# Reciprocal square roots moved from VectorE to GpSimd in a two-block transformer kernel

## The chip, the cores and the metric

One core of a Trainium2 chip runs the whole kernel. The metric is the device time of one execution in microseconds (us), as the median of several runs. The engines are named as in the profile: PE is TensorE's matmul, PEld its weight load, DVE is VectorE, ACT is ScalarE, POOL is GpSimd and SP is SyncE, which here only issues DMAs. Each engine takes its instructions in one fixed order; an instruction whose input is not ready holds up all that stand behind it on the same engine.

## What is computed

Two transformer blocks on one sequence of 1024 tokens with 1024 features, in float32. The first has a hybrid mixer (a gated MLP over positions, differential attention, top-k sparse attention) and a feed-forward part of width 2816, with layer norms; the second has stick-breaking attention and a pooling mixer, the same feed-forward width, and RMS norms with a modulation. All the norms need one reciprocal square root for each token:

```
def layer_norm(x, g, b):
    mu = jnp.mean(xf, axis=-1, keepdims=True)
    xc = xf - mu
    var = jnp.mean(xc * xc, axis=-1, keepdims=True)
    return xc * lax.rsqrt(var + LN_EPS) * g + b

def rms_norm(x, g):
    ms = jnp.mean(xf * xf, axis=-1, keepdims=True)
    return xf * lax.rsqrt(ms + LN_EPS) * g
...
x = layer_norm(DEEPNORM_ALPHA * x + mix @ w_out, ln1_g, ln1_b)
ffn = (silu(gate) * up) @ w_down
x = layer_norm(DEEPNORM_ALPHA * x + ffn, ln2_g, ln2_b)
```

## The kernel before

A float32 matrix product is made of three products of a high and a low part (`mm3`, L95 to L99). A `split` (L79 to L84) makes those parts: a cast on ACT (L80) and a subtraction on DVE or POOL (L84). Tokens go in eight blocks of 128, a token to a partition. The program is handed to a scheduler, which lays out each engine's order from a timeline of its own (L1699), so taking instructions off one engine reorders others too.

`rsqrt(v, n)` (L101) takes the reciprocal root of n columns by a shift and a subtraction on the bits of the number (L105, L106), a scaling (L107) and three Newton steps (L110 and L114 for one column; L112, L113 and L114 for eight). It is called 56 times:

- eight times with eight columns, in the first 500 us: four in the gated MLP (L437), four in the differential attention (L596);
- 24 times with one column by the two layer norms and `modulate1`: `norm_stats` (L852) calls it for `layer_norm` (L863), eight for the norm after the first mixer ("norm1" below, about 595 to 695 us) and eight for the one after the first feed-forward part ("after1", about 1355 to 1450 us); in after1 `rms_scale` (L873) is called once more for each block by `modulate1` (L1245);
- 24 times with one column by `rms_scale` in the second block: two for each token block in `norm2` (L1460, about 1830 to 1950 us), one for each in `after2` (L1589, from 2584 us to the end).

What stands around it for one token block: in a layer norm a `shift` of one column (L866, DVE), the scaling of the block (L867, ACT), and a product and a sum with gain and bias (L868, L869), by the block on POOL or DVE. In `norm2` a product with a gain on POOL (L1466 for the first five blocks, L1472 for the last three), the sum with the residual on DVE (L1473), the second root, and a scaling on ACT (L1476). After that the block goes to `SAct.put` (L810): PE transposes it (L817), and the parts are split (L807 on ACT, L808 on DVE). `sums` (L829) forms differences of those parts on POOL and DVE (L834 to L836, L846, L847), which PE needs for the products of the feed-forward part. In `after2` the product with the gain is L1598, on POOL but for the last block, and the final sum is L1601 on DVE. Between the norms PE runs the products of the stage (L694 to L696 of the output projection, L97 to L99 of the feed-forward part), with their sums on DVE (L721, L1191).

Of the kernel before, what the change touches and what calls it, by code (L numbers as in the profile page):

```python
# [9 lines left out]
F32 = mybir.dt.float32  # L10
# [3 lines left out]
I32 = mybir.dt.int32  # L14
U32 = mybir.dt.uint32
AF = mybir.ActivationFunctionType
OP = mybir.AluOpType
# [6 lines left out]
P = 128  # L24
NB = S // P
# [13 lines left out]
def two_blocks(ctx: ExitStack, tc: tile.TileContext, a):  # L39
    nc = tc.nc  # L40
    V, A, T, G, DMA = nc.vector, nc.scalar, nc.tensor, nc.gpsimd, nc.sync

    cst = ctx.enter_context(tc.tile_pool(name="cst", bufs=1))
# [5 lines left out]
    def pool(name, side="left"):  # L49
        st = ExitStack()  # L50
        return st.enter_context(tc.tile_pool(name=name, bufs=1, side=side, reuse_waits="tile")), st
# [43 lines left out]
    def mm3(out, lh, ll, rh, rl, start, stop, more=False):  # L95
# [2 lines left out]
        T.matmul(out, lh, rl, start=False, stop=False, skip_group_check=more)  # L98
        T.matmul(out, ll, rh, start=False, stop=stop, skip_group_check=more)  # L99

    def rsqrt(v, n):  # L101

        y = sml.tile([P, n], F32, tag=f"rs{n}", name="rs_y")
        t = sml.tile([P, n], F32, tag=f"rt{n}", name="rs_t")
        V.tensor_single_scalar(t.bitcast(I32), v.bitcast(I32), 1, op=OP.logical_shift_right)  # L105
        V.tensor_scalar(y.bitcast(I32), t.bitcast(I32), -1.0, 1597463007.0, op0=OP.mult, op1=OP.add)  # L106
        V.tensor_single_scalar(v, v, -0.5, op=OP.mult)  # L107
        for _ in range(3):
            if n == 1:
                V.scalar_tensor_tensor(t, y, v, y, op0=OP.mult, op1=OP.mult)  # L110
            else:
                V.tensor_tensor(t, y, y, op=OP.mult)  # L112
                V.tensor_tensor(t, t, v, op=OP.mult)  # L113
            V.scalar_tensor_tensor(y, t, 1.5, y, op0=OP.add, op1=OP.mult)  # L114
        return y

    def row(t, src):
# [114 lines left out]
    def key_chunks(L):  # L232
        return (1, max(L, 256)) if L <= 512 else (2, L // 2)
# [176 lines left out]
    def gmlp_pieces():  # L410
# [10 lines left out]
        for q in range(4):  # L421
            vg = xpool.tile([P, 2, 256], F32, tag="stg", bufs=4, name="vg")
            for t in range(2):
                o = gemm_tm(wv, q * 2 + t, 256)
                with soon():
                    A.activation(vg[:, t, :], o, AF.Gelu_apprx_tanh)
            v3 = vg.rearrange("p t (g c) -> p (t g) c", c=64)
            mu = sml.tile([P, 8], F32, tag="mu", name="mu")
            V.reduce_sum(mu, v3, axis=AX.X)
            V.tensor_single_scalar(mu, mu, 1.0 / 64.0, op=OP.mult)  # L430
            V.tensor_tensor(v3, v3, mu[:, :, None].to_broadcast([P, 8, 64]), op=OP.subtract)
            sq = xpool.tile([P, 8, 64], F32, tag="stg", bufs=4, name="sqv")
            A.activation(sq, v3, AF.Square)
            va = sml.tile([P, 8], F32, tag="va", name="va")
            V.reduce_sum(va, sq, axis=AX.X)
            V.tensor_scalar(va, va, 1.0 / 64.0, LN_EPS, op0=OP.mult, op1=OP.add)
            rs = rsqrt(va, 8)  # L437
            V.tensor_tensor(v3, v3, rs[:, :, None].to_broadcast([P, 8, 64]), op=OP.mult)
            G.tensor_tensor(vg, vg, lng[:, None, :].to_broadcast([P, 2, 256]), op=OP.mult)
            G.tensor_tensor(vg, vg, lnb[:, None, :].to_broadcast([P, 2, 256]), op=OP.add)  # L440
            DMA.dma_start(vn_d[:, q * 2:q * 2 + 2, :], vg)
            yield
# [28 lines left out]
    for blk in SCORED:  # L471
        L = (blk + 1) * P
        nch, n = key_chunks(L)
# [73 lines left out]
    class LaneB:  # L547
# [30 lines left out]
        def mix(self):  # L578
            h, i = divmod(self.m, NB)
            if i == 0:  # L580
                self.vt = p1.tile([P, NB, P], F32, tag="v", bufs=1, name="vB")
                DMA.dma_start(self.vt, bv_d[:, :, h * P:(h + 1) * P])
                self.ot = p1.tile([P, NB, P], F32, tag="o", bufs=2, name="oB")
            e0, r0 = self.e.pop(self.m)
            po = probs_v(e0, i, self.vt, P, (1, 2), ps_mm)
            ot = self.ot
            V.tensor_scalar_mul(ot[:, i, :], po, r0)
            self.m += 1
            if i < NB - 1:
                return  # L590
            sq = p1.tile([P, NB, P], F32, tag="o", bufs=2, name="sqB")
            G.tensor_tensor(sq, ot, ot, op=OP.mult)
            va = sml.tile([P, NB], F32, tag="vb", name="vb")
            V.reduce_sum(va, sq, axis=AX.X)
            V.tensor_scalar(va, va, 1.0 / P, LN_EPS, op0=OP.mult, op1=OP.add)
            rs = rsqrt(va, NB)  # L596
            V.tensor_tensor(ot, ot, rs[:, :, None].to_broadcast([P, NB, P]), op=OP.mult)
            G.tensor_tensor(ot, ot, subg[:, None, :].to_broadcast([P, NB, P]), op=OP.mult)
            DMA.dma_start(mix_d[:, :, 256 + h * P:256 + (h + 1) * P], ot)
# [53 lines left out]
    accp, _ = pool("accp", "right")  # L653
# [198 lines left out]
    def norm_stats(x):  # L852

        st = sml.tile([P, 2, 6], F32, tag="bst", name="bst")
        for c in range(2):
            V.bn_stats(st[:, c, :], x[:, c * 512:(c + 1) * 512])
        mv = sml.tile([P, 2], F32, tag="mv", name="mv")
        V.bn_aggr(mv, st)
        va = sml.tile([P, 1], F32, tag="va1", name="va1")
        V.tensor_scalar_add(va, mv[:, 1:2], LN_EPS)  # L860
        return mv[:, 0:1], rsqrt(va, 1)
# [719 lines left out]
    n = 0  # L1581
# [121 lines left out]
```

## Time and profile before

| what | value |
|---|---|
| time, median of 3 runs | 2641.62 us (2641.22 to 2645.37) |
| the profiled execution's own time | 2638.86 us |
| its span in the trace | 2637.0 us |
| mean granted clock of TensorE, of full speed | 0.954 |
| PE busy | 2398.2 us, 91% |
| DVE busy | 1889.9 us, 72% (3300 instructions) |
| ACT busy | 1083.0 us, 41% |
| POOL busy | 931.7 us, 35% (550 instructions) |

The span is what the trace covers; the execution's own time is a little longer, since some start and end lies outside it. Busy shares are means over stages in which different engines are waited for, so they do not say by themselves which engine sets the time at a given place; the rows further down are of single stages.

### The profile page before, as it was taken

How to read it: one execution, taken by the hardware profiler on the slowest of the kernel's cores; microseconds unless marked ns; L12 is line 12 of the kernel's file. 1: busy time of each engine (PE TensorE's matmuls, PEld its weight loads, DVE VectorE, ACT ScalarE, POOL GpSimd, SP SyncE). 2: the span in 40 equal slices, each digit the busy share in tenths (PEclk: the TensorE clock that was granted, in tenths of full speed). 3: DMA queues.
4: the chain of work that ended last, by engine and by line, in shares of the span. 5: the costliest groups of instructions: out<-in, count | busy, mean ns of one | idle time of the engine just before them, and what ended most of it. 6: DMA issues, size and time to landing. Idle time of an engine off the chain costs nothing. (4 is left out here: it accounts for less than half of the span.)

```text
span 2637.0 us, 32552 instructions
## 1 busy us (share of the span) xinstructions
PE 2398.2 (91%) x11584; PEld 1963.6 (74%) x11584; DVE 1889.9 (72%) x3300; ACT 1083.0 (41%) x1893; POOL 931.7 (35%) x550
## 2 busy tenths in 40 slices
PE   8889897898799999989987989898879999998997
PEld 8878776787677777867866878687657788876875
DVE  4889869648866777679987366667974555548997
ACT  4559774343223223333336334445642332225332
POOL 2220233115612222356542042426361222227634
PEclk9999998999899999999998999999989999999998
DMA  5154355423254444262303524562511222214313
GB/s 181 57 150 119 115 160 168 112 83 110 97 171 135 153 168 156 86 246 80 128 16 136 163 84 139 150 180 73 183 65 57 75 80 85 76 61 175 120 66 110
DMA packets 149789, 314.32 MB, mean 119 GB/s; under 512 B 19574, under 2 KB 65654, under 8 KB 149628
## 3 DMA queue, kind: packets, MB, share of 16 engines
q1 hardware_dynamic: 139260, 293.38, 34.4%
q10 hardware_dynamic: 10368, 18.88, 1.9%
q8 instruction: 91, 1.49, 0.2%
q14 instruction: 70, 0.57, 0.1%
HBM read 230.39 MB, written 81.81 MB: 118 GB/s over the span
## 5 line engine op out<-in xcount | busy, mean ns | idle before, releaser
L940 ACT CAST wst<-tt 128x512 fp32r<-128x512 f32 x144 | 89.2, 621 | 252.7 <-PE plg L99 206.8
L941 POOL TENSOR_TENSOR wst<-rw,wst 128x512 fp32r<-128x512 f32 x51 | 74.6, 1463 | 269.2 <-ACT wst L940 97.3
L84 POOL TENSOR_TENSOR wl<-raw,wh 128x1024 fp32r<-128x1024 f32 (+2 forms) x28 | 66.9, 2393 | 243.8 <-ACT wh L80 215.2
L339 PE MATMUL plg<-qk,qk 128*128 128x384 f32 (+4 forms) x480 | 124.5, 375 | 19.9 <-DVE mn L352 6.3
L97 PE MATMUL plg<-ws,hs 128*128 128x512 f32 x288 | 114.6, 398 | 5.4 <-ACT dacc L1158 2.9
L1505 DVE TENSOR_TENSOR_SCAN sab<-sab 128x640 f32<-128x640 f32 (+7 forms) x64 | 102.0, 1599 | 19.0 <-ACT sab L1503 18.3
L280 ACT ACTIVATE junk_a<-xi,cand 128x1024 bf16<-128x1024 f32 (+1 forms) x124 | 108.8, 878 | 14.9 <-DVE cand L269 6.8
L98 PE MATMUL plg<-ws,hs 128*128 128x512 f32 x288 | 113.9, 395 | 0.0
L99 PE MATMUL plg<-ws,hs 128*128 128x512 f32 x288 | 113.8, 395 | 0.0
L941 DVE TENSOR_TENSOR wst<-tt,wst 128x512 fp32r<-128x512 f32 x144 | 107.6, 749 | 8.4 <-ACT wst L940 7.8
L339 PEld LDWEIGHTS plg<-qk,qk 128*128 128x128 f32 x480 | 81.2, 196 | 30.7 <-DVE mn L352 9.1
L84 POOL TENSOR_TENSOR hs<-hr,hs 128x1024 fp32r<-128x1024 f32 (+1 forms) x30 | 69.0, 2301 | 83.6 <-ACT hs L80 70.2
L1214 DVE SCALAR_TENSOR_TENSOR mod<-raw_c,sc,mod 128x1024 f32<-128x1024 f32 x42 | 57.6, 1371 | 54.3 <-DMA raw_c<-in_w_cond_dram 54.2
L963 DVE TENSOR_TENSOR u<-plg,u 128x512 f32<-128x512 f32 x36 | 24.8, 690 | 97.4 <-PE plg L99 97.4
L164 PE MATMUL pmm<-wh,xh 128*128 128x256 f32 (+1 forms) x320 | 91.5, 286 | 3.1 <-DVE stgl L401 1.8
L940 ACT CAST wst<-rw 128x512 fp32r<-128x512 f32 x77 | 47.6, 618 | 111.1 <-PE plg L99 56.8
L353 ACT ACTIVATE e<-e,mn 128x128 f32<-128x128 f32 (+7 forms) x96 | 74.1, 773 | 46.1 <-DVE mn L352 42.3
L165 PE MATMUL pmm<-wl,xh 128*128 128x256 f32 (+1 forms) x320 | 90.5, 283 | 0.0
L166 PE MATMUL pmm<-wh,xl 128*128 128x256 f32 (+1 forms) x320 | 90.5, 283 | 0.0
L989 POOL TENSOR_TENSOR u<-u,u 128x512 f32<-128x512 f32 x36 | 54.9, 1526 | 92.6 <-issue 54.9
L80 ACT CAST wh<-raw 128x1024 fp32r<-128x1024 f32 x54 | 56.4, 1047 | 72.1 <-PE pmm L98 28.2
L694 PE MATMUL pmm<-woh,mixh 128*128 128x512 f32 x192 | 79.9, 416 | 6.6 <-DVE rs_t L110 2.1
(566 smaller groups left out, 8459.4 us busy)
## 6 DMA issues: line engine op xcount, KB each, us to landing
raw_c<-in_w_cond_dram SPq DMA_DIRECT2D x48, 512.0 KB, 4.0
hr<-h_d SPq DMA_DIRECT2D x44, 512.0 KB, 4.2
wr<-in_w_down_dram SPq DMA_DIRECT2D x44, 512.0 KB, 4.2
qk<-qkd SPq DMA_DIRECT2D x72, 256.0 KB, 5.7
rw<-in_wgu_dram SPq DMA_DIRECT2D x36, 512.0 KB, 4.6
x_d<-acc SPq DMA_DIRECT2D x24, 512.0 KB, 2.9
qk<-qk2d SPq DMA_DIRECT2D x48, 256.0 KB, 4.8
raw<-in_wqk_dram SPq DMA_DIRECT2D x20, 512.0 KB, 5.1
```

Of the source, the lines that this page charges most:

```text
L84: eng.tensor_tensor(lo, src, hi.bitcast(F32), op=OP.subtract)
L97: T.matmul(out, lh, rh, start=start, stop=False, skip_group_check=more)
L98: T.matmul(out, lh, rl, start=False, stop=False, skip_group_check=more)
L99: T.matmul(out, ll, rh, start=False, stop=stop, skip_group_check=more)
L164: T.matmul(o, at(0, k, tb * P, P), h[:, j, :], start=(k == 0), stop=False)
L165: T.matmul(o, at(0, k, tb * P, P), l[:, j, :], start=False, stop=False)
L166: T.matmul(o, at(1, k, tb * P, P), h[:, j, :], start=False, stop=(k == KT - 1))
L280: A.activation(junk_a[:, :L], xi[self.blks[i]], AF.Sign, bias=c, accum_out=self.cnt[:, i:i + 1])
L339: T.matmul(pl[:, c, :n], q[:, isl], k2[:, c * n:(c + 1) * n], start=(j == 0), stop=last)
L940: A.copy(wh, x)
L941: (G if p in (2, 4) else V).tensor_tensor(wl, x, wh.bitcast(F32), op=OP.subtract)
L1505: V.tensor_tensor_scan(sa[:, ::-1], sa[:, ::-1], sa[:, ::-1], 1.0, op0=OP.mult, op1=OP.bypass)
```

## The change

`rsqrt` no longer uses DVE. A column of -0.5 is set once (`mhalf`, a POOL memset), and the root is a power on POOL, followed by one Newton step in four small POOL operations, for one column and for eight alike. It has five instructions where there were nine on DVE for one column and twelve for eight. The lines behind it move up by two.

```
+    mhalf = cst.tile([P, NB], F32, name="mhalf")
+    G.memset(mhalf, -0.5)
+
     def rsqrt(v, n):
         y = sml.tile([P, n], F32, tag=f"rs{n}", name="rs_y")
         t = sml.tile([P, n], F32, tag=f"rt{n}", name="rs_t")
-        V.tensor_single_scalar(t.bitcast(I32), v.bitcast(I32), 1, op=OP.logical_shift_right)
-        V.tensor_scalar(y.bitcast(I32), t.bitcast(I32), -1.0, 1597463007.0, op0=OP.mult, op1=OP.add)
-        V.tensor_single_scalar(v, v, -0.5, op=OP.mult)
-        for _ in range(3):
-            if n == 1:
-                V.scalar_tensor_tensor(t, y, v, y, op0=OP.mult, op1=OP.mult)
-            else:
-                V.tensor_tensor(t, y, y, op=OP.mult)
-                V.tensor_tensor(t, t, v, op=OP.mult)
-            V.scalar_tensor_tensor(y, t, 1.5, y, op0=OP.add, op1=OP.mult)
+        G.tensor_tensor(y, v, mhalf[:, :n], op=OP.pow)
+        G.tensor_tensor(t, y, y, op=OP.mult)
+        G.tensor_tensor(t, t, v, op=OP.mult)
+        G.tensor_scalar(t, t, -0.5, 1.5, op0=OP.mult, op1=OP.add)
+        G.tensor_tensor(y, y, t, op=OP.mult)
         return y
```

In the changed kernel the power is L108 and the step L109 to L112. The order of the instructions changes with them, as three places show.

The first place is the end of norm1. Before, DVE works on the root of the seventh token block (its variance is `va_6672`) between the large operations of `sums` and of the splits:

```order
L105 TENSOR_SCALAR rs_t<-va_6672 128x1
L856 BN_STATS bst<-acc 128x6
L836 TENSOR_TENSOR tt<-tt,x1B12l 128x512
L106 TENSOR_SCALAR rs_y<-rs_t 128x1
L107 TENSOR_SCALAR va_6672<-va_6672 128x1
L721 TENSOR_TENSOR acc<-acc,pmm 128x512
L84 TENSOR_TENSOR wl<-raw,wh 128x1024
L846 TENSOR_TENSOR tt<-x1B22h,tt 128x512
L110 SCALAR_TENSOR_TENSOR rs_t<-rs_y,va_6672 128x1
L84 TENSOR_TENSOR wl<-raw,wh 128x1024
...
L114 SCALAR_TENSOR_TENSOR rs_y<-rs_t,rs_y 128x1
```

In the changed kernel POOL has the same block's root (there `va_6594`) between the last layer-norm sum of the block ahead (L867 there) and the operations of `sums` that POOL has anyway:

```order
L108 TENSOR_TENSOR rs_y<-va_6594,mhalf 128x1
L867 TENSOR_TENSOR acc<-acc,ln1b 128x1024
L833 TENSOR_TENSOR tt<-tt,x1B12l 128x512
L109 TENSOR_TENSOR rs_t<-rs_y 128x1
L834 TENSOR_TENSOR tt<-tt,x1B11l 128x512
L110 TENSOR_TENSOR rs_t<-rs_t,va_6594 128x1
L111 TENSOR_SCALAR rs_t<-rs_t 128x1
L112 TENSOR_TENSOR rs_y<-rs_y,rs_t 128x1
...
L833 TENSOR_TENSOR tt<-tt,x1B12l 128x512
L108 TENSOR_TENSOR rs_y<-va_6656,mhalf 128x1
L866 TENSOR_TENSOR acc<-acc,ln1g 128x1024
L834 TENSOR_TENSOR tt<-tt,x1B11l 128x512
L109 TENSOR_TENSOR rs_t<-rs_y 128x1
```

So the seventh block's root has three large POOL operations inside it, and the eighth's (`va_6656`) two, of which one (L866) is the product of the seventh block.

The second place is the last token block of `norm2`, where two roots follow each other; in the changed kernel POOL has:

```order
L108 TENSOR_TENSOR rs_y<-ss,mhalf 128x1
L833 TENSOR_TENSOR tt<-tt,x3B12l 128x512
L111 TENSOR_SCALAR rs_t<-rs_t 128x1
L109 TENSOR_TENSOR rs_t<-rs_y 128x1
L834 TENSOR_TENSOR tt<-tt,x3B11l 128x512
L112 TENSOR_TENSOR rs_y<-rs_y,rs_t 128x1
L110 TENSOR_TENSOR rs_t<-rs_t,ss 128x1
...
L833 TENSOR_TENSOR tt<-tt,x3B12l 128x512
L108 TENSOR_TENSOR rs_y<-ss,mhalf 128x1
L834 TENSOR_TENSOR tt<-tt,x3B11l 128x512
L109 TENSOR_TENSOR rs_t<-rs_y 128x1
L110 TENSOR_TENSOR rs_t<-rs_t,ss 128x1
```

Here the first of its two roots is interleaved with another block's root and with two large operations of `sums` (L833, L834), and the second has one of these inside it (L834).

The third place is the end of the program. Before, DVE's last rows are the root of the last block and the final sum:

```order
L877 TENSOR_SCALAR ss<-ss 128x1
L1601 SCALAR_TENSOR_TENSOR acc<-fg,rs_y,x3r 128x1024
L105 TENSOR_SCALAR rs_t<-ss 128x1
L106 TENSOR_SCALAR rs_y<-rs_t 128x1
L107 TENSOR_SCALAR ss<-ss 128x1
L110 SCALAR_TENSOR_TENSOR rs_t<-rs_y,ss 128x1
L114 SCALAR_TENSOR_TENSOR rs_y<-rs_t,rs_y 128x1
```

After, POOL's last rows are:

```order
L1596 TENSOR_TENSOR fg<-acc,gpf 128x1024
L108 TENSOR_TENSOR rs_y<-ss,mhalf 128x1
L109 TENSOR_TENSOR rs_t<-rs_y 128x1
L110 TENSOR_TENSOR rs_t<-rs_t,ss 128x1
L111 TENSOR_SCALAR rs_t<-rs_t 128x1
L112 TENSOR_TENSOR rs_y<-rs_y,rs_t 128x1
L108 TENSOR_TENSOR rs_y<-ss,mhalf 128x1
```

The roots of the last two blocks follow each other there without a large POOL operation between them.

## Rows read from the trace of the kernel before

**Rows 1.** Windows: length, busy time of each engine, PEclk, DMA share, GB/s.

```profile
595.00:695.00 100.00, 78.14 (x351) 62.25 (x350) 87.09 (x176) 31.05 (x45) 53.53 (x27) 0.88 0.30 106
1355.00:1450.00 95.00, 79.32 (x338) 62.33 (x338) 79.14 (x248) 51.84 (x83) 33.14 (x14) 0.91 0.29 106
1830.00:1950.00 120.00, 88.55 (x386) 68.77 (x386) 111.29 (x260) 70.54 (x134) 58.28 (x33) 0.86 0.35 117
1920.00:1950.00 30.00, 11.26 (x35) 7.78 (x35) 28.53 (x44) 15.81 (x33) 19.34 (x13) 0.60 0.07 26
```

**Rows 2.** DVE's groups of instructions by line: busy us, mean ns, idle before.

```profile
L114 DVE SCALAR_TENSOR_TENSOR rs_y<-rs_t,rs_y 128x1 f32<-128x1 f32 (+1 forms) x168 | 55.1, 334 | 2.1
...
L110 DVE SCALAR_TENSOR_TENSOR rs_t<-rs_y,ss 128x1 f32<-128x1 f32 x96 | 32.6, 345 | 1.1
```

**Rows 3.** Timeline of POOL and DVE in norm1: start us, us, instruction.

```profile
606.40 2.39 POOL L868 TENSOR_TENSOR acc<-acc,ln1g 128x1024 f32<-128x1024 f32 x1 [37.77 <-ACT acc L867]
608.87 2.39 POOL L869 TENSOR_TENSOR acc<-acc,ln1b 128x1024 f32<-128x1024 f32 x1
608.97 2.31 DVE L110 SCALAR_TENSOR_TENSOR rs_t<-rs_y,va 128x1 f32<-128x1 f32 x1
```

**Rows 4.** Timeline of POOL and DVE, last two blocks of norm1.

```profile
656.04 1.63 POOL L835 TENSOR_TENSOR tt<-tt,x1B12l 128x512 f32<-128x512 f32 x1
656.44 0.14 DVE L105 TENSOR_SCALAR rs_t<-va 128x1 int32<-128x1 int32 x1
672.94 0.14 DVE L105 TENSOR_SCALAR rs_t<-va 128x1 int32<-128x1 int32 x1
674.66 0.15 DVE L866 SCALAR_TENSOR_TENSOR shift<-mv,rs_y 128x1 f32<-128x1 f32 x1
678.55 0.16 DVE L866 SCALAR_TENSOR_TENSOR shift<-mv,rs_y 128x1 f32<-128x1 f32 x1
678.62 1.22 DVE L869 TENSOR_TENSOR acc<-acc,ln1b 128x1024 f32<-128x1024 f32 x1
```

**Rows 5.** PE's waits, three stretches: total us, times, longest.

```profile
PE ptr L817 <- DVE acc L869: 12.6, 1, 12.6
...
PE ptr L767 <- DVE rs_y L114: 5.2, 1, 5.2
...
PE ptr L817 <- DVE x3B12l L808: 11.3, 2, 7.1
PE plg L97 <- ACT x3B11h L807: 6.7, 1, 6.7
PE plg L97 <- ACT x3B12h L807: 6.1, 1, 6.1
```

**Rows 6.** PE's longest wait for DVE in the differential attention, 250 to 500 us.

```profile
PE pmm L374 <- DVE e L371: 13.0, 3, 5.7
```

**Rows 7.** Timeline of DVE, last block of norm2.

```profile
1912.04 0.14 DVE L105 TENSOR_SCALAR rs_t<-ss 128x1 int32<-128x1 int32 x1
...
1918.75 0.15 DVE L114 SCALAR_TENSOR_TENSOR rs_y<-rs_t,rs_y 128x1 f32<-128x1 f32 x1
...
1923.13 0.15 DVE L105 TENSOR_SCALAR rs_t<-ss 128x1 int32<-128x1 int32 x1
...
1930.89 0.15 DVE L114 SCALAR_TENSOR_TENSOR rs_y<-rs_t,rs_y 128x1 f32<-128x1 f32 x1
```

**Rows 8.** Timeline of POOL and DVE in after2.

```profile
2592.12 2.40 POOL L1598 TENSOR_TENSOR fg<-acc,gpf 128x1024 f32<-128x1024 f32 x1 [3.65 <-DVE acc L1191]
2598.14 2.40 POOL L1598 TENSOR_TENSOR fg<-acc,gpf 128x1024 f32<-128x1024 f32 x1 [3.61 <-DVE acc L1191]
...
2630.68 0.15 DVE L105 TENSOR_SCALAR rs_t<-ss 128x1 int32<-128x1 int32 x1
...
2632.26 0.16 DVE L114 SCALAR_TENSOR_TENSOR rs_y<-rs_t,rs_y 128x1 f32<-128x1 f32 x1
```

**Rows 9.** POOL's small copies in the stick-breaking stage: ns, min/median/max.

```profile
L1378 POOL COPY pw<-pu x4: 187/188/1077, 1531.3 to 1649.2; 128x1 f32<-128x1 f32 x4
```

## The prediction

> **What bounds the kernel now.** I read the windows first, for the five places where roots are taken, because means over the whole span hide what a stage waits for. In norm1 DVE is busy 87.09 of 100 us and PE 78.14; in after1 both are near 79 of 95; in norm2 DVE has 111.29 of 120 against 88.55 for PE, and in norm2's last 30 us it has 28.53 while PE has 11.26, at a granted clock of 0.60 [rows 1]. So in the norms DVE is the fuller engine, and POOL has room: 53.53 of 100, 33.14 of 95 and 58.28 of 120. Then I read PE's waits for these stretches. The longest are 12.6 us in norm1, until the last layer-norm sum L869 is there; 5.2 us in after1, until a root's last L114; and in norm2 11.3, 6.7 and 6.1 us for parts of the last token blocks (L808, L807), which follow from two roots in a row [rows 5]. The reader is to see that these waits end at a chain that runs through `rsqrt`, though the name in the row is mostly that of a later step. Outside the norms, PE's longest wait for DVE where roots lie is in the differential attention, 13.0 us in three pieces for L371 [rows 6].
>
> Then DVE's groups: L114 takes 55.1 us in 168 instructions, mean 334 ns, and the larger group of L110 has a mean of 345 ns [rows 2]. For one column that is far too much, and the timeline says why. While POOL runs L869 (2.39 us from 608.87), an L110 on DVE that begins at 608.97 takes 2.31 us and ends just when POOL does [rows 3]; an L105 that begins under POOL's L835 takes 0.14 [rows 4]. A small DVE operation with two operands waits out a POOL operation of two operands; one with a single operand doesn't.
>
> **The change, part by part.**
>
> *Removed.* 48 calls of nine operations and eight of twelve, 528 DVE instructions. In norm2 it is 16 x 3 x (0.334 + 0.345) = 32.6 us for L110 and L114 alone [rows 2], out of DVE's 111.29 [rows 1]. It counts only where it stands in a chain that PE waits for.
>
> *Added.* 56 x 5 POOL operations and a memset at the start, which lies under the first loads. The cheapest POOL operation of this shape that the trace has is a copy of one column: 0.19 us, with a maximum of 1.08 [rows 9]. Between dependent POOL operations there is a gap of 0.08 us (606.40 + 2.39 to 608.87) [rows 3]. Four small operations are then 4 x (0.19 + 0.08) = 1.08 us, and the power comes to p + 0.08. No row has a power. Its bounds are 0.19, since it can hardly be cheaper than a copy, and 2.39, a whole operation of 1024 columns and two operands [rows 3]. It is one column, so it is nearer to the copy; a power has many inner steps, so I take four copies, p = 0.8. A root is then 0.88 + 1.08 = 2.0 us on POOL (bounds 1.35 and 3.55). On DVE, undisturbed, the last one takes 2630.68 to 2632.42 = 1.74 us [rows 8]. In itself the root gets a little slower. What can be won is that it no longer queues behind DVE's large operations and isn't held up by POOL's, for it now stands on POOL itself. A page speaks against the change: by the Trainium skill, "GPSIMD Engine Reference", section "Engine selection", elementwise work belongs on VectorE and GpSimd is about half as fast with two inputs. The trace agrees for 1024 columns: L869 took 2.39 us on POOL and 1.22 on DVE [rows 3, 4]. By that rule five operations of twice DVE's 0.16 us [rows 8] with the gaps would be 2.0 us, no other sum.
>
> *POOL's load.* Sixteen roots add 32 us to 58.28 of 120 in norm2 and to 33.14 of 95 in after1, eight add 16 to 53.53 of 100 in norm1 [rows 1]: POOL doesn't fill up, but it also keeps its order, and each root can stand behind or around a large POOL operation. So I priced the chains with what the order has inside them.
>
> *norm1.* Before, the seventh block's root lasted from L105 at 656.44 to the shift L866 at 674.66, 18.2 us, since DVE did all its other work in between; the eighth's lasted from 672.94 to 678.55, 5.6 us, and PE waited 12.6 us for what follows it [rows 4, 5]. After, the seventh has one operation of 2.39 us and two of 1.63 inside: 0.8 + 2.39 + 3.26 + 1.08 = 7.5 us. The eighth has one of each: 0.8 + 2.39 + 1.63 + 1.08 = 5.9. So 10.7 us are won on the seventh and 0.3 lost on the eighth. The wait depends on the eighth, whose statistics start earlier when DVE is freer, but whose chain now holds the product of the seventh. I take half of the wait, 6.3 us; bounds 0 and 12.6.
>
> *after1.* The 5.2 us were a wait for a root itself [rows 5]. Two roots for each block have moved and POOL is the emptiest here. I take half, 2.6; bounds 0 and 5.2.
>
> *norm2.* The last block's two roots lasted from 1912.04 to 1918.90, 6.9 us, and from 1923.13 to 1931.04, 7.9 us [rows 7]. After, the first has two operations of 1.63 us and three small ones of another root inside: 0.8 + 3.26 + 1.08 + 0.8 = 5.9. The second has one of 1.63: 3.5. Won are 1.0 + 4.4 = 5.4 us, on a chain that sets PE's waits of 6.7 and 6.1. Bounds: 0, if the blocks' sums on DVE or ACT's squares are late next, and all three waits, 24.1.
>
> *The end.* The last root is on the path to the last output: 2.0 for 1.74, a loss of 0.3. Bounds are -1.8 (3.55) and +0.4 (1.35). In the steady stretch of after2, POOL's product L1598 comes every 6.0 us and takes 2.40 [rows 8], so 3.6 us for a root are free.
>
> *The first 500 us.* Eight roots of eight columns leave DVE, where each was at least 12 x 0.16 = 1.9 us by the undisturbed L114 [rows 8]. PE's 13.0 us for L371 [rows 6] are a wait for DVE, though not for a root. The order of the whole stage is laid out anew. I take 2 us. Upper bound 13.0; lower -6.6, half of 8 x (3.55 - 1.9).
>
> The sum: 2 + 6.3 + 2.6 + 5.4 - 0.3 = 16.0 us. From the profiled execution's 2638.86 that leaves 2622.9. The median of the runs is 2641.62, 2.8 higher, so I predict 2625.6. The bounds add to -8.4 (2650) and +55.3 (2586).
>
> **The rivals.**
>
> *The power is dear (slower).* If p is near its upper bound or over it, POOL becomes the fuller engine. In norm2 that is so from 16 x (p + 1.16) + 58.28 = 120, p = 2.7; in after2 from p + 1.16 = 3.6, p = 2.4. With p = 3.5 norm2 needs 16 x 4.66 + 58.28 = 132.8 us, 13 more; after1 74.6 + 33.1 = 107.7, 13 more than 95; after2 8 x 1.06 = 8 more, and the last root 2.9. That is 37 us and about 2679. For it: no row has the operation. Against: one column is little for any engine. Chance 0.12.
>
> *POOL's order binds (slower).* With p as I take it, a root that waits for its input (the square sum of ACT) holds up POOL's large operations behind it, or one of 2.39 us stands before a root that PE waits for. At one such operation in four of the 24 one-column roots of the second block it would be 6 x 2.4 = 14, less 4 won elsewhere: 2652. The order at the end of norm1 (a product inside the eighth root) speaks for it, POOL's share against. Chance 0.06.
>
> *The contention comes along (slower).* Small POOL operations with two operands might wait out DVE's large ones as DVE's waited out POOL's. If each second of the four were held up by one of 1.22 us [rows 4], a root would be 2.0 + 2.4 = 4.4 us; norm2 would need 16 x 4.4 + 58.28 = 128.7, 9 over its 120, after1 103.5, 9 over 95, and the last root 2.7 more: 20.7 us and about 2662. It decides from about one operation in three. For it: one of the four copies of one column took 1.08 us instead of 0.19 [rows 9]. Against: L868, with no stalled DVE beside it, and L869, with a stalled one, both took 2.39, so POOL lost nothing there [rows 3]. The Trainium skill, "GPSIMD Engine Reference", section "Key points", says that GpSimd shares its SBUF interfaces with VectorE, with contention where a DVE instruction has two SBUF inputs; it doesn't say which of the two waits. Chance 0.05.
>
> *Nothing comes of it.* The roots get shorter, but PE's waits pass on to the next in line: statistics, casts and sums on DVE, which still has 111.29 - 32.6 us in norm2 plus what the new order puts there. 2640. Chance 0.15.
>
> *More comes of it.* The waits of the last blocks go almost whole: 12.6 + 5.2 + 24.1 = 41.9, and as PE rests less, the stretch at 0.60 of the clock [rows 1] shrinks; at nine tenths that is 38 us and 2604. Chance 0.10.
>
> **How the numbers follow.** My forecast has 0.52, with a range of its own from 2610 to 2634: 2625.6 with half the sum lost or doubled. 0.2% is 5.3 us, about what a measurement of this kernel can tell from no change. Faster is the forecast and "more", 0.62; same is "nothing", 0.15; slower is the dear power, the bound order and the contention, 0.23. The range from 2606 to 2652 leaves out the dear power, the contention and some of "more", together about 0.2.
>
> **What would show it.** Right: DVE's L114 and L110 gone and no small DVE operation of 2.3 us in the norms; the power's row at 0.4 to 1.5 us and a root of two to three; PE's wait in norm1 at half of 12.6 and those of norm2 for L807 shorter. Wrong: a power of more than 2.4 us; POOL near full in norm2; large POOL operations waiting for a power or for its input; or the same waits of PE with a sum on DVE as the releaser, which would be "nothing". A shift of more than 6 us in the first 500 us, either way, would say that the new order and not the roots set the time.

## The result and the profile after

The changed kernel takes 2607.98 us (median of 4 runs, 2606.26 to 2614.44), the kernel before 2642.60 on the same footing (4 runs, 2641.22 to 2645.37). The ratio is 0.9876, with a 95% interval from 0.9858 to 0.9894: 1.24% or some 33 us faster. 2625.6 us was forecast, 16 us faster. The sign was right and the gain is twice the forecast. The range of 2606 to 2652 held by 2 us only, and the narrower one that the prediction gives to the forecast itself, 2610 to 2634, was missed. The profiled execution of the changed kernel took 2614.44, the longest of the four, against 2638.86 before, so the two traces show 24 of the 33 us. The ratios here and below are of undisturbed executions: one execution of `n1_only`, the profiled one, whose trace is therefore not used, took 4670 us for an unknown cause, and one of `pow_rms_pool` 2712.57 us at a granted clock of 0.83; the medians in the tables count both.

The new instructions come first, in the view of POOL's lines that use the root's tile: ns at least, in the median and at most, and when the first and last began.

```profile
L109 POOL TENSOR_TENSOR rs_t<-rs_y x56: 187/194/1032, 73.7 to 2606.7; 128x1 f32<-128x1 f32 x48, 128x8 f32<-128x8 f32 x8
L112 POOL TENSOR_TENSOR rs_y<-rs_y,rs_t x56: 184/191/962, 75.4 to 2607.6; 128x1 f32<-128x1 f32 x48, 128x8 f32<-128x8 f32 x8
L108 POOL TENSOR_TENSOR rs_y<-ss,mhalf x32: 540/550/1460, 1363.3 to 2606.1; 128x1 f32<-128x1 f32 x32
...
L108 POOL TENSOR_TENSOR rs_y<-vb,mhalf x4: 1641/1648/3017, 276.5 to 471.3; 128x8 f32<-128x8 f32 x4
```

A power of one column takes 0.55 us, where 0.8 was assumed, and a power of eight columns 1.65, which the sum had not priced apart. The small operations take 0.19 as in the copy of [rows 9]. The timeline of the last root, which answers to the end of [rows 8]:

```profile
2606.10 0.55 POOL L108 TENSOR_TENSOR rs_y<-ss,mhalf 128x1 f32<-128x1 f32 x1 [2.06 <-DVE ss L875]
2606.73 0.19 POOL L109 TENSOR_TENSOR rs_t<-rs_y 128x1 f32<-128x1 f32 x1
2607.00 0.19 POOL L110 TENSOR_TENSOR rs_t<-rs_t,ss 128x1 f32<-128x1 f32 x1
2607.28 0.19 POOL L111 TENSOR_SCALAR rs_t<-rs_t 128x1 f32<-128x1 f32 x1
2607.55 0.19 POOL L112 TENSOR_TENSOR rs_y<-rs_y,rs_t 128x1 f32<-128x1 f32 x1
2607.78 1.41 DVE L1599 SCALAR_TENSOR_TENSOR acc<-fg,rs_y,x3r 128x512 f32<-128x512 f32 x2 [1.76 <-POOL rs_y L112]
```

From 2606.10 to 2607.74 it lasts 1.64 us, against 1.74 on DVE. So undisturbed the root is about as long as before, and the loss of 0.3 for its length did not come. The same four windows as in [rows 1]:

```profile
595.00:695.00 100.00, 76.80 (x349) 61.13 (x348) 82.28 (x107) 31.86 (x45) 76.95 (x72) 0.88 0.30 106
1355.00:1450.00 95.00, 84.29 (x425) 70.17 (x423) 55.96 (x107) 58.26 (x100) 51.86 (x89) 0.93 0.35 122
1830.00:1950.00 120.00, 93.92 (x411) 74.17 (x410) 88.71 (x114) 71.13 (x131) 87.86 (x118) 0.87 0.38 126
1920.00:1950.00 30.00, 22.54 (x84) 17.48 (x84) 26.09 (x23) 10.05 (x17) 24.55 (x16) 0.77 0.14 40
```

DVE falls from 79.14 to 55.96 us in after1 and from 111.29 to 88.71 in norm2, and PE rises there; in norm1 DVE falls by 5 only, and PE doesn't rise. (The work has moved by up to 15 us in these windows, so they compare stages and not instructions.) PE's waits, in the stretches of [rows 5]:

```profile
PE plg L97 <- ACT wh L80: 10.4, 1, 10.4
PE ptr L815 <- DVE acc L867: 8.5, 1, 8.5
...
PE ptr L765 <- DVE x20l L777: 6.5, 3, 4.9
PE ptr L765 <- ACT x21h L776: 3.2, 1, 3.2
...
PE ptr L815 <- DVE x3B12l L806: 7.9, 2, 6.9
PE ptr L815 <- DVE ss L875: 5.2, 1, 5.2
PE plg L97 <- ACT x3B12h L805: 4.8, 1, 4.8
```

The waits named in the prediction shrank or went (12.6 to 8.5; 11.3 to 7.9; the 5.2 for a root; 6.7 and 6.1 to 4.8), and new ones stand beside them, above all 10.4 us for a cast of weights in norm1.

**Where the time lies.** For this table each matmul of the kernel before was paired with the one of the same line, tiles and number in the other trace; a figure is by how many us it starts earlier (-) or later (+) there, as the median over the 20 us ahead of the time named in the first column. The runs are those of the next section.

```
before, us  after  c_after  five_dve  load_dve  no_newton  pow_x4  const_only
 140         -2.1    -1.7     -2.4      -0.7      -3.5     +20.8     +1.2
 500         -7.1   -10.8     -9.4      -9.6     -10.4      +9.0     -1.2
 595         -2.3    -6.0     -7.8      -9.6      -8.9     +12.7     -1.5
 700         -2.4    -6.0    -14.3      -3.4     -18.7     +12.1     -1.3
1345         -5.9    -3.6     -9.2      -5.2     -19.5     +13.7     -0.5
1450        -14.8   -12.7    -16.0      -9.5     -34.9     +29.7     -1.7
1830         -7.6    -6.2    -14.5      +1.3     -28.8     +33.0     -0.9
1950        -15.3   -15.0    -19.8      +1.1     -37.2     +48.1     -0.2
2395        -19.9   -20.1    -21.1      -2.4     -41.1     +44.6     -3.5
2640        -23.6   -23.3    -26.1      -4.7     -46.3     +39.5     -3.9
```

Read the second column downwards: of 7.1 us won by 500, 4.8 are given back by 595; nothing is won across norm1 (595 to 700), 3.5 us up to after1, 8.9 in after1 (1345 to 1450), 7.7 in norm2 (1830 to 1950), 4.6 in the gate-up products behind it, which take no root, and 3.7 in the rest. In the stick-breaking stage (1450 to 1830) 7.2 are lost again. The first two columns are two executions of one program, and they differ by up to 3.7 us (at 500 and 595), so a step of a few us between two rows of one trace can be chance.

**What norm1's gain went into.** In norm1 PE's waits did not get less: they add to 21.9 us before and 23.2 after. Before, a second one stood beside the 12.6 us, which no term of the prediction has, and it is gone:

```profile
PE ptr L682 <- DVE rs_t L105: 6.4, 1, 6.4
```

The 12.6 us were a wait for the seventh block's sum and not for the eighth's, as the prediction took it: the L869 of [rows 4], at 678.62, is the seventh block's, and DVE makes the eighth's only after it. That one, then PE's transposes of the two blocks with the product between them, before:

```profile
682.45 1.22 DVE L869 TENSOR_TENSOR acc<-acc,ln1b 128x1024 f32<-128x1024 f32 x1 [2.60 <-POOL acc L868]
```

```profile
679.99 1.94 PE L817 MATMUL ptr<-ident,acc 128*128 128x128 f32 x8 [12.64 <-DVE acc L869]
683.54 0.79 PE L97 MATMUL plg<-x1B11h,wh 128*128 128x512 f32 x1 [1.61 <-ACT wh L80]
...
691.67 1.03 PE L817 MATMUL ptr<-ident,acc 128*128 128x128 f32 x8
```

In the changed kernel the seventh block's transposes start at 667.61 instead of 679.99, 12.4 us earlier, 2.3 of them won ahead of norm1, and the eighth's at 680.95 instead of 691.67. But the product between them starts at 679.93 instead of 683.54:

```profile
667.61 1.94 PE L815 MATMUL ptr<-ident,acc 128*128 128x128 f32 x8 [8.55 <-DVE acc L867]
679.93 0.79 PE L97 MATMUL plg<-x1B11h,wh 128*128 128x512 f32 x1 [10.38 <-ACT wh L80]
...
680.95 1.93 PE L815 MATMUL ptr<-ident,acc 128*128 128x128 f32 x8
```

ACT's and DVE's timelines say why the cast is late:

```profile
678.32 0.62 ACT L805 CAST x1T3h<-tt 128x512 fp32r<-128x512 f32 x1 [5.74 <-DVE tt L834]
678.84 1.04 ACT L80 CAST wh<-raw 128x1024 fp32r<-128x1024 f32 x1
...
673.90 2.71 DVE L833 TENSOR_TENSOR tt<-tt,x1B22l 128x512 f32<-128x512 f32 x1
676.65 1.63 DVE L834 TENSOR_TENSOR tt<-tt,x1B12l 128x512 f32<-128x512 f32 x1
```

In ACT's new order the cast of the weights (L80) stands behind the cast of `x1T3h`, and ACT sits 5.74 us until DVE's L834 is there. Before, the same cast began at 682.45, but PE was late itself and waited only 1.6 us for it. POOL's roots were also longer here than forecast. The root of the seventh block:

```profile
644.75 1.00 POOL L108 TENSOR_TENSOR rs_y<-va,mhalf 128x1 f32<-128x1 f32 x1
645.72 2.41 POOL L867 TENSOR_TENSOR acc<-acc,ln1b 128x1024 f32<-128x1024 f32 x1
648.09 1.75 POOL L833 TENSOR_TENSOR tt<-tt,x1B12l 128x512 f32<-128x512 f32 x1
649.79 0.64 POOL L109 TENSOR_TENSOR rs_t<-rs_y 128x1 f32<-128x1 f32 x1
650.39 1.29 POOL L834 TENSOR_TENSOR tt<-tt,x1B11l 128x512 f32<-128x512 f32 x1
651.63 1.17 POOL L110 TENSOR_TENSOR rs_t<-rs_t,va 128x1 f32<-128x1 f32 x1
652.89 0.19 POOL L111 TENSOR_SCALAR rs_t<-rs_t 128x1 f32<-128x1 f32 x1
653.17 0.19 POOL L112 TENSOR_TENSOR rs_y<-rs_y,rs_t 128x1 f32<-128x1 f32 x1
```

It lasts 8.6 us (7.5 forecast, 18.2 before on DVE), with the large operations inside that the order had shown. A power of 1.00 and an L110 of 1.17 instead of 0.19 show that POOL's small operations get stretched as well as DVE's do.

### The profile page after: what moved, and what is told of

Read it like the earlier page. It is cut to its first block, busy times and chain, and to the rows that moved or that the text cites. A ratio compares the mean times of both kernels' runs of the same rounds, so it can differ in the third digit from the quotient of the medians.

```text
span 2612.7 us, 32305 instructions
## 1 busy us (share of the span) xinstructions
PE 2385.6 (91%) x11584; PEld 1962.2 (75%) x11584; DVE 1791.0 (69%) x2772; ACT 1083.4 (41%) x1893; POOL 1031.4 (39%) x831
## 3 DMA queue, kind: packets, MB, share of 16 engines
q1 hardware_dynamic: 139260, 293.38, 35.4%
## 4 chain that ended last, share of the span: by engine, by line
PE 40%; DVE 4%; POOL 3%; issue 3%; ACT 2%; DMA 2%; SPq 0%; DVEq 0%; ACTq 0%; POOLq 0%
PE plg L97 5%; PE plg L98 5%; PE plg L99 5%; PE pmm L97 5%; PE pmm L98 5%; PE pmm L99 5%; PE ptr L98 1%; PE ptr L99 1%; PE ptr L97 1%; PE plg L337 1%; POOL last L84 1%; DVE sab L1503 1%; PE ptr L1525 1%; PE pmm L692 1%; PE pmm L693 1%
## 5 line engine op out<-in xcount | busy, mean ns | idle before, releaser
L80 ACT CAST wh<-raw 128x1024 fp32r<-128x1024 f32 x54 | 56.5, 1050 | 73.2 <-PE pmm L98 30.8
L97 PE MATMUL pmm<-xh,wh 128*128 128x512 f32 x192 | 79.3, 413 | 7.4 <-DVE oB L585 4.8
```

Of the source, the lines that this page charges most:

```text
L97: T.matmul(out, lh, rh, start=start, stop=False, skip_group_check=more)
```

## The experiments

Theory Q is the prediction's: the root leaves DVE's queue, and that is the gain. All twelve runs are here, in three groups that ran on one chip each. A time in us under or over before is the distance of the ratio from 1, times 2641. Each run but the control is a program of its own for the scheduler. `const_only` and `const_64` keep every engine's order of before, and `five_const` that of `five_dve`; in all others the order of the instructions changes too, on PE as well.

**The control, five operations on DVE, and the two halves.**

`c_after` is the changed kernel again. `five_dve` leaves all on DVE with one Newton step:

```
-        for _ in range(3):
+        for _ in range(1):
```

`n1_only` and `n8_only` choose the new code by `n == 1` or `n == 8` and the old one for the rest.

> The changed kernel once more, as a control on this chip. Theory Q (the root leaves DVE's queue and is then no longer held up there): the ratio to before is again 0.988, some 2610 us, and the gains lie at the same places of the program as in the first trace: about 5 us in after1, 8 in norm2, 3 in after2. Rival N (part of the gain is noise of a single execution): the 6 us that were gained inside the second gate-up products, 1950 to 2400 us, where no root is taken, don't come back, since PE's pace there is 234 ns for one matmul again and not 232.

> All roots stay on DVE with one Newton step instead of three: five operations for one column as in the change, but on DVE (six for eight columns). The root is less exact by that. Rival C (the gain comes from the smaller number of operations, the engine doesn't matter): nearly all of the gain, 25 us or more. Theory Q: the remaining operations still queue behind DVE's large ones and behind two-operand operations of POOL, so a root loses four of nine steps and the kernel gains about four ninths of 33 us, 10 to 18 us.

> Only the 48 roots of one column are moved to POOL; the eight of eight columns stay on DVE as before. Theory Q: all but some 2 us of the gain stays, so about 30 us under before, 2612. Rival O (the new order of the attention stages matters as much as the roots): the time differs from the changed kernel by more than 6 us either way.

> Only the eight roots of eight columns are moved to POOL; the 48 of one column stay on DVE as before. Theory Q and the prediction's term: 2 us under before, within 5. Rival O: more than 6 us under or over before. With the control and the run that moves only the 48, the two gains should add up to the whole if the places are independent of each other.

| run | median us | ratio to before (95%) | under before |
|---|---|---|---|
| c_after | 2613.41 | 0.9894 (0.9876 to 0.9912) | 28.0 |
| five_dve | 2604.52 | 0.9866 (0.9848 to 0.9883) | 35.4 |
| n1_only | 2619.22 | 0.9914 (0.9893 to 0.9935) | 22.7 |
| n8_only | 2628.20 | 0.9952 (0.9935 to 0.9969) | 12.7 |

The control repeats the gain and the table's steps in the norms, and the 4.6 us of the second gate-up products (5.1 there): rival N is out, that part is no noise of one execution. It does not repeat the 3.5 us ahead of after1, where it loses 2.4. `five_dve` decides against theory Q as it was put: with no root moved at all, and only fewer operations on DVE, the kernel gains as much as by the move. Rival C had said so. `n8_only` misses its expectation: 12.7 us, not 2. `n1_only` has 22.7 where some 30 were expected. The two halves add to 35.4 us; both have the column of `mhalf`, which the next group prices at 5.8, and counted once that leaves 29.6, near the control's 28.0.

**A column that nobody reads, seven operations, the power alone, the power four times.**

`const_only` adds the two lines of `mhalf` to the kernel before and leaves its roots alone. `seven_dve` has `range(2)` in the line above. `pow_x4` has the line with the power four times. `no_newton` stops after it:

```
         G.tensor_tensor(y, v, mhalf[:, :n], op=OP.pow)
-        G.tensor_tensor(t, y, y, op=OP.mult)
-        G.tensor_tensor(t, t, v, op=OP.mult)
-        G.tensor_scalar(t, t, -0.5, 1.5, op0=OP.mult, op1=OP.add)
-        G.tensor_tensor(y, y, t, op=OP.mult)
```

> The kernel before with only the column of -0.5 and its memset added; the roots stay as they were, and nothing reads the column. Theory L (the column moves every tile that is placed after it, and PE's pace in the gate-up products hangs on that): 0.2324 us from one matmul to the next in the second gate-up products instead of 0.2343, 0.2328 instead of 0.2334 in the first, and 4 to 7 us under before, 2634 to 2637. Rival (the pace comes from what runs beside PE once the roots are gone): the pace stays at 0.2343 and the time at that of before.

> All roots on DVE with two Newton steps instead of three: seven operations for one column where there were nine (nine for twelve with eight columns); the root is a little less exact by that. Theory K (what counts is how many operations a root has in its chain, on either engine): half of what one step on DVE gave, 13 to 22 us under before, 2618 to 2627. Rival (only the new order of the schedule counts, with no law in it): any time between 2600 and 2645, with no relation to the number of steps.

> The changed kernel without the Newton step: a root is the power alone, one POOL operation of 0.55 us for one column; it is as exact as the power is. Theory K: the chain loses about 1.05 us of 1.6 in each of 56 roots, a dozen of which PE waits for, so 8 to 15 us under the changed kernel, about 2598. Theory Q (once the root has left DVE its length matters little): within 5 us of the changed kernel, 2606 to 2616.

> The changed kernel with the power taken four times in a row, the same result each time: a root of one column lasts 1.6 + 3 x 0.6 = 3.4 us on POOL, as with a power of 2.4, the upper bound of the prediction. Theory K: a dozen roots that PE waits for, 1.8 us each, so 15 to 25 us over the changed kernel, near 2630. Theory Q: within 6 us of the changed kernel, since POOL still has room in each stage.

| run | median us | ratio to before (95%) | under or over before |
|---|---|---|---|
| const_only | 2635.59 | 0.9978 (0.9966 to 0.9990) | -5.8 |
| seven_dve | 2630.64 | 0.9957 (0.9941 to 0.9973) | -11.4 |
| no_newton | 2589.69 | 0.9806 (0.9789 to 0.9823) | -51.2 |
| pow_x4 | 2677.41 | 1.0138 (1.0120 to 1.0156) | +36.4 |

`const_only` shows that 5.8 us (2.6 to 9) can be had with no change to a root. The view is that of the windows, PE alone, from 2030 to 2330 us, inside the second gate-up products: length, PE busy with its matmuls, granted clock, DMA share, GB/s. One line each of before, after, `const_only` and `five_dve`:

```profile
2030.00:2330.00 300.00, 299.76 (x1280) 1.00 0.22 80
```

```profile
2030.00:2330.00 300.00, 300.00 (x1293) 1.00 0.23 80
```

```profile
2030.00:2330.00 300.00, 299.76 (x1290) 1.00 0.23 80
```

```profile
2030.00:2330.00 300.00, 300.00 (x1282) 1.00 0.23 80
```

PE is busy all the time at the full clock in all four, yet it gets 1290 matmuls or more through where the column exists, and 1280 or 1282 where it doesn't. Pairing the same 1278 matmuls takes the shift of the windows out: over these 300 us PE gets ahead of the kernel before by 2.4 us in all nine traced runs with the column of 32 bytes, `pow_x4` among them, and by nothing in `five_dve` and `seven_dve`. In `const_only` every engine has its instructions in the order of before, so the order is not the cause. The column takes 32 bytes in each partition, and tiles that are placed after it move by that. This is the cause that remains; no address was traced. From the trace of `const_only` to that of the changed kernel PE's busy time stays the same (2386.1 and 2385.6 us) and the span is 20.4 us shorter, so what the roots add to the column there is time in which PE had waited.

`no_newton` and `pow_x4` show that the chain on POOL counts after all: 1.09 us less for each root is worth about 20 us against the changed kernel, and 1.9 us more costs about 67. Both lie beyond what theory K had given them (8 to 15 less, 15 to 25 more). `pow_x4` loses from the start: 20.8 us by 140 us, in the gated MLP, where its four powers of eight columns stand one behind the other:

```profile
70.74 1.67 POOL L108 TENSOR_TENSOR rs_y<-va,mhalf 128x8 f32<-128x8 f32 x1 [9.80 <-DVE va L437]
72.48 1.65 POOL L109 TENSOR_TENSOR rs_y<-va,mhalf 128x8 f32<-128x8 f32 x1
74.21 1.64 POOL L110 TENSOR_TENSOR rs_y<-va,mhalf 128x8 f32<-128x8 f32 x1
75.93 2.05 POOL L111 TENSOR_TENSOR rs_y<-va,mhalf 128x8 f32<-128x8 f32 x1
```

The table still has 12.7 of these at 595 us, so that much of its loss comes from the roots of eight columns. It loses 16 us in after1 and 15 in norm2 too, though POOL isn't full there; its windows for those two stages, in which its work lies 14 to 48 us later than before:

```profile
1350.00:1450.00 100.00, 73.41 (x295) 56.57 (x293) 50.14 (x95) 38.03 (x60) 81.85 (x129) 0.83 0.11 42
1830.00:1950.00 120.00, 93.02 (x436) 75.19 (x435) 69.58 (x97) 66.18 (x118) 92.91 (x129) 0.86 0.41 130
```

`seven_dve` gains a third of what `five_dve` does, a little less than the lower end of its expectation; the direction fits theory K, the law is not a straight line, and its rival, an effect of the order with no law, is not excluded by this run.

**DVE loaded again, the column added to `five_dve`, a wider column, one more step off DVE.**

`load_dve` adds to the changed kernel nine small DVE operations for each root, on scratch columns:

```
+        V.tensor_single_scalar(z.bitcast(I32), v.bitcast(I32), 1, op=OP.logical_shift_right)
+        V.tensor_scalar(q.bitcast(I32), z.bitcast(I32), -1.0, 1597463007.0, op0=OP.mult, op1=OP.add)
+        V.tensor_single_scalar(z, v, -0.5, op=OP.mult)
+        for _ in range(3):
+            V.scalar_tensor_tensor(z, q, 0.0, q, op0=OP.mult, op1=OP.mult)
+            V.scalar_tensor_tensor(q, z, 1.0, q, op0=OP.add, op1=OP.mult)
```

`five_const` is `five_dve` with the two lines of `mhalf`, `const_64` is `const_only` with `2 * NB` values, and `pow_rms_pool` is `no_newton` with `G` for `V` in the line that scales the square sum in `rms_scale`.

> The changed kernel with nine small operations put back on DVE for each root, of the same kinds as those that the change removed, on a scratch column that nobody reads: DVE has as many instructions as before, but the chain to the root is the short one on POOL. Theory K (the length of the root's own chain is what counts): within 6 us of the changed kernel, 2604 to 2616. Rival D (DVE is relieved of 528 instructions, and that is the gain): at least half of the gain is lost again, 2625 or more.

> One Newton step on DVE, as in the run with five operations there, and the unused column of -0.5 added. If the place of the tiles is an effect of its own, it comes on top: 4 to 7 us under the run without the column, about 2599, with 0.2324 us from one matmul to the next in the second gate-up products. Rival: no faster than the run without the column, for the order is another one.

> The kernel before with an unused column block of twice the width (16 values of -0.5 for each partition, 64 bytes where the change adds 32); the roots as before. If any shift of the tiles quickens the gate-up products, PE's pace in the second of them is 0.2324 us again; if only some shifts do, it is 0.2343 as in the kernel before, and the time that of before.

> The power alone as the root, as in the run without the Newton step, and the scaling of the square sum ahead of it (the mean and the small constant) moved from DVE to POOL too, in the RMS norms. Their chain then runs from ACT to POOL with no step in DVE's queue: one DVE operation less in 32 chains, one POOL operation of 0.2 us more. Theory K with the queue of DVE in the chain: 3 to 10 us under the power alone, 2580 to 2587. Rival (DVE's step was not waited for): the same within 4 us.

| run | median us | ratio to before (95%) | under before |
|---|---|---|---|
| load_dve | 2632.11 | 0.9957 (0.9941 to 0.9973) | 11.4 |
| five_const | 2603.69 | 0.9848 (0.9832 to 0.9865) | 40.1 |
| const_64 | 2636.51 | 0.9976 (0.9964 to 0.9988) | 6.3 |
| pow_rms_pool | 2594.25 | 0.9810 (0.9792 to 0.9829) | 50.2 |

`load_dve` is the run that bears most on the main question. Its roots are those of the changed kernel, on POOL, and nobody needs the scratch columns; yet it keeps 11.4 us of some 30, and 5.8 of these are what the column gives. Theory K had said that it stays within 6 us of the changed kernel; rival D, that at least half is lost. D is right. The roots themselves have not become longer: from the power to L112 one lasts 4.93 us in the mean in norm1 (4.97 in the changed kernel), 3.06 in after1 (3.03) and 3.58 in norm2 (3.68). DVE's busy time is 1869.0 us, so 78.0 of the 98.9 us that the change took off it are back. The scratch operations stall on DVE as the root's did, with 341 and 262 ns in the mean (before: 345 and 334, [rows 2]), and what stands behind them in DVE's order comes late. Its groups for these, and norm2's window:

```profile
L119 DVE SCALAR_TENSOR_TENSOR rs_z<-rs_q 128x1 f32<-128x1 f32 (+1 forms) x168 | 55.6, 341 | 1.9
...
L120 DVE SCALAR_TENSOR_TENSOR rs_q<-rs_z,rs_q 128x1 f32<-128x1 f32 (+1 forms) x168 | 42.5, 262 | 1.9
```

```profile
1830.00:1950.00 120.00, 87.76 (x388) 69.02 (x385) 106.30 (x261) 71.65 (x135) 76.55 (x113) 0.86 0.36 120
```

PE is back at 87.76 busy us in norm2 (before 88.55, after 93.92) and DVE at 106.30. In the table norm2 wins nothing in this run, norm1 loses 6.2 and after1 gains 4.3 instead of 8.9. Its matmuls have the quick pace (1291 in the 300 us above), so the place of the tiles is not what it loses by. Two things limit the reading. The first 500 us keep all of their gain (9.6) with the scratch operations there as well, so DVE's relief is not what wins in that stretch. And PE's order is another one than in the changed kernel at some 1700 of 11584 places; no run changes the order alone, so its part in the loss is not shown.

`five_const` is 4.7 us under `five_dve` by the ratios, as the column alone would have it, but the two intervals overlap. Its trace says more: in the order of `five_dve`, the matmuls have the quick pace again, 1292 where `five_dve` has 1282:

```profile
2030.00:2330.00 300.00, 300.00 (x1292) 1.00 0.22 78
```

`const_64` is faster than before too, though its matmuls are only half quickened (1285 in the same 300 us, 1.2 us ahead in the pairing): not every shift does the same. `pow_rms_pool` is no faster than `no_newton`: moving DVE's scaling step gains nothing. `no_newton` is the fastest of all kernels here, 1.9% under the kernel before and some 20 us under the changed one, with the power alone as the root.

## Why the prediction was right in sign and half in size

*DVE is the fuller engine in the norms, and its small operations stall under POOL.* Right. Putting the operations back on DVE with nobody waiting for them takes most of the gain away while the roots on POOL stay as long (`load_dve`); that the order is another one there too is the one rival that no run takes out.

*"What can be won is that it no longer queues behind DVE's large operations."* This was the reason given for the move, and it is half of the matter only. Five operations left on DVE gain as much (`five_dve`). What wins besides, by `load_dve`, is that DVE, the engine that the norms wait for, has fewer of these stalling operations, for all that stands behind them. The move relieves DVE by 98.9 us of busy time (1889.9 to 1791.0), `five_dve` by 58.8 (to 1831.1), and still gains no less. The move pays for a chain on POOL: with about the same relief, `no_newton` (1783.0) and `pow_x4` (1787.3) end 51 us under and 36 us over before. How much of the gain of `five_dve` is relief and how much its shorter chain, no run tells apart.

*The power at 0.8, a root of 2.0 us.* Measured 0.55 and 1.64, for one column. This step was close.

*norm1, 6.3 us.* The largest term, and worth nothing: net 0.1 us, and 0.0 in the control. The step took the 12.6 us for a wait for the eighth block and so halved it; it was one for the seventh, whose root did get shorter, nearly as forecast (18.2 to 8.6 us, with 7.5 forecast). Those transposes came 12.4 us earlier, and the next wait took it: ACT's new order put a cast of weights behind one that waits for DVE. "The waits pass on", the rival of no change, was true of this stage. That it is the order and not the roots is argued from the traces: `five_dve`, with another order, keeps 6.5 there, and `no_newton` 9.8.

*after1, 2.6 us, and norm2, 5.4 us.* Measured 8.9 and 7.7, in the control 9.1 and 8.8. In after1 one wait of PE was taken as the bound, but DVE fell there by 23 us; this is the term that was sized worst. Behind it 7.2 us are given back in the stick-breaking stage, in nearly every run where after1 gained (6.5, 1.5, 6.1 and 10.8 in the control, `five_dve`, `no_newton` and `load_dve`), by no single wait that the trace names. That stays open.

*The end, -0.3.* The root is 0.1 us shorter instead of 0.3 longer. Down products and after2 together give 3.7.

*The first 500 us, 2 us.* `n8_only` measures 12.7, of which 5.8 are the column's: some 7, with an uncertainty of the same size. The traces have 2 to 8 at 595 us. Under-sized, within its bounds. At 500 us the change is 7.1 us ahead and the control 10.8, which meets the prediction's own sign that the new order and not the roots set the time there; `load_dve`, as far ahead with DVE loaded again, fits that, and no run takes it further.

*Missing from the sum: the place of the tiles.* The memset "lies under the first loads", the prediction said of the constant; its time does, but the column itself is worth 5.8 us.

*The sum.* It was right in sign although its largest term came to nothing: after1 and norm2 brought 8.6 us more than they were given, and the place of the tiles, for which the prediction had no reason, 5.8 more. That the time still lies in the range is in part luck.

*The rivals.* The dear power was a true danger, with the wrong threshold. The prediction let it decide from p = 2.4 to 2.7, where POOL would be full. `pow_x4`, with 2.4 us for the power, is at +36 already, with POOL at 92.91 of 120 us in norm2; a third of this is there by 595 us, with the eight-column roots. On a straight line through two points, the control (28 under at 0.55) and this run, the change would be worth nothing from a power of about 1.4 us on, by estimate; the chain's length costs long before the engine is full. "The contention comes along" is true in part (1.17 for 0.19 in norm1, and DVE's large L833 at 2.71 beside POOL's product, where it takes 0.69 at least). The Trainium skill, page "GPSIMD Engine Reference", section "Engine selection", prefers VectorE for elementwise work. At an equal count of five that holds here: `five_const` (five on VectorE) is at 40.1 us under before, the control with five on GpSimd at 28.0, both with the column; the five on VectorE have one Newton step and no power, so by their arithmetic they are less exact.

## What to carry to other kernels

When an engine that a stage waits for holds many tiny operations, count what they do to everything queued behind them, and not only the chain that they form; a run with the same operations put back for nobody is a direct test of that, as far as the scheduler's order stays the same. Before moving them, try to have fewer of them: taking out operations won as much as moving them, and both together won most. This kernel gained 5.8 us from tiles that moved by 32 bytes, and what a remade order is worth by itself was not measured, so a control that changes only these belongs beside a small result. And before a wait is priced, find the one instruction that ends it: the largest term here was built on the wrong token block.

## What the runs showed that was not expected

A power on POOL takes 0.55 us for 128x1 and 1.65 for 128x8. A column of 32 bytes for each partition that nobody reads raised the matmuls in 300 us of a stage that PE fills from 1280 to 1290 at a granted clock of 1.00, and one of 64 bytes to 1285. One of POOL's small two-operand operations was stretched from 0.19 to 1.17 us in norm1, as DVE's had been.
